# Spacing the first recurrence unit of an encoder kernel, and fixing the place of four scalings in ScalarE's order

## The chip, the cores and the metric

The kernel runs on one core of a Trainium2 chip. The metric is device time in microseconds (us) from the start to the end of one execution. Before the change three runs took 2597.24, 2600.26 and 2603.55 us; the median, 2600.26 us, is the time before.

The engines are named as in the profile: PE is TensorE (matmuls), PEld its weight loads, DVE is VectorE, ACT is ScalarE, POOL is GpSimd, and SP issues the DMAs. Each engine works through its own queue of instructions in order, and waits on semaphores for what other engines produce.

## The reference

One layer of an encoder: 2048 tokens of width 1024, all in float32. What is computed, cut to its core:

```python
h = layernorm(x) * (1 + scale) + shift            # scale, shift, gate from silu(c) @ ada_w + ada_b
proj = h @ w_in                                   # 1024 x 9216
q_h, i_h, zf_fw, zf_bw, g_h, q_n, k_n, v_n, g_n = split(proj)
y_hg = hgrn2(q_h, i_h, zf_fw, zf_bw, g_h)         # gated linear recurrence in both directions, 8 heads of 128
y_na = neighbourhood_attention(q_n, k_n, v_n) * silu(g_n)   # 16 heads of 64
x = layernorm(alpha * x + gate * (concat(y_hg, y_na) @ w_out)) * ln_g + ln_b
```

In the recurrence a state S follows S_t = diag(f_t) S_(t-1) + k_t v_t^T with k = 1 - f, and the output is o_t = S_t^T q_t, once forward and once backward over the tokens.

## The kernel before

**Dense products.** Every product with `w_in` is made of three matmuls in a reduced 32-bit format (line 278): the high part of the weights with the high and the low part of the activations, and the low part of the weights with the high part. One dense *step* is the three matmuls of one 128-row slice of the contraction for one output block of 128 columns by 512 tokens (`proj_mm`); eight steps fill a block. The block then leaves PSUM by a copy or an exponential on ACT (lines 379, 384, 389, 782, 299 and so on), from a pool `pj` of two buffers, so that a block two further on cannot start before that copy. Weights come by DMA into `wr`, ACT rounds them to the high part `wh` (line 268 or 833), DVE subtracts to get the low part `wl` (line 269 or 834). There are four buffers of each.

**Phases that matter here.** After the start, the first half of the tokens (groups 0 and 1 of 512) goes through neighbourhood attention for eight head pairs (`first_half`). Within it, the tokens of the second half (groups g = 0 and 1 of `rows`, `stats`, `scale`, `piece`) are loaded, normalised, transposed and stored for later. This work is laid out by hand in 32 slots, four to a head pair: for g = 0 the loads are in slot 11, the statistics in 12, the two scalings (a = 0 and a = 1, the left and right 512 columns) in 13 and 14, and the eight pieces, which transpose (line 232) and split, from slot 14 on, pieces 0 to 3 using a = 0 and pieces 4 to 7 using a = 1. For g = 1 the statistics and the first scaling are in slot 23, the second scaling and the first piece in 24. One scaling is four instructions: rows 0 and 1 on ACT (line 225), rows 2 and 3 on DVE (line 227).

Then comes the recurrence: 16 units (two token halves by eight heads u), each of two groups g of 512 tokens. While a unit's recurrence is worked, the dense products of the next unit are woven into it.

**What sets the order.** PE's order is the order in which the program is written. `weave` takes a generator of the recurrence (`hgrn`) and one of dense steps; at every `yield w` of the first it issues dense steps until their share of the total has reached the share of the weights so far (a unit has 54 in weights and 80 steps). So the numbers in the `yield` lines 583 to 619 say how many dense steps PE does between two parts of the recurrence. In group 0 of the first unit these are 8, 7, 5, 4, 9 and 8 steps for the weights 5, 5, 3, 3, 6 and 5.

In the two phases above the orders of ACT, DVE and SP are not written out. A planner makes them when the program is built, with costs of its own for every instruction: of what is ready it takes the instruction with the smallest priority number, which is its place in the program, less `PRI` = 1500 inside `tc.high_priority(offset=PRI)`. A change in PE's order therefore makes the plan anew from that point on. `pinned(ins)` adds one rule: `ins` is put behind the instruction that was written last before it on its own engine. In `first_half` the weight roundings of line 833 and the attention's score reductions of line 1065 are so pinned.

**A group of the recurrence, in order.** `turned(vts)` transposes the values; `rates` (ACT and DVE) makes log rates and their running sums for both directions; `ends` makes the factors `de`; `turned(de)` transposes on PE (line 474) and ACT copies the result to `ke` (line 476); `updates(ke, v)` (line 482) makes the state updates, forward then backward; `diagonal_factors` makes `kx` and `qx` (lines 506 to 512), and `diagonal` (line 521) 64 small matmuls with them; `level_factors` and `level` (line 549) do the same for the blocks further from the diagonal; `masked` copies the level's result to `pm` on ACT (line 555), copies the diagonal's result through masks into `pd` on DVE (line 559), and adds the two on DVE (line 562); `outputs` (lines 573 and 575) multiplies with the values and the states.

Of the kernel before, what the change touches and what calls it, by code (L numbers as in the profile page):

```python
# [13 lines left out]
AF = mybir.ActivationFunctionType  # L14
# [16 lines left out]
PRI = 1500  # L31
# [7 lines left out]
def body(ctx: ExitStack, tc: tile.TileContext, t):  # L39
    nc = tc.nc  # L40
    dve, act, pool, pe = nc.vector, nc.scalar, nc.gpsimd, nc.tensor
    dma = nc.sync.dma_start
    x, out = t["x"], t["out"]
# [44 lines left out]
    def nm(s):  # L88
        cnt[0] += 1
        return f"{s}_{cnt[0]}"  # L90

    def tl(tag, dt=F32, shape=None):
        if tag in cur["smap"]:
            tag = cur["smap"][tag]
            return sh.tile([P, 512], dt, tag=tag, name=nm(tag), bufs=SH[tag])
        return cur["pool"].tile([P, 512] if shape is None else shape, dt, tag=tag, name=nm(tag), bufs=cur["bufs"].get(tag, 1))

    def short(dt=F32):
        return tl("s", dt)

    def ps(tag="mx"):
        if tag == "pj":
            return pp.tile([P, 512], F32, tag=tag, name=nm("pj"))
        tag = cur["map"].get(tag, tag)
        return cur["psum"].tile([P, 512], F32, tag=tag, name=nm("ps"), bufs=cur["ps"][tag])
# [109 lines left out]
    def x_stats(xs, pin=lambda x: x):  # L215
        mv = x_mv()
        for i in range(4):
            x_stat(mv, xs, i, pin)
        return x_rates(mv)

    def x_scale(xs, how, a, on_act=2, rows=range(4)):
        mv, r, b = how
        for i in rows:
            if i < on_act:
                act.activation(xs[i][a], xs[i][a], AF.Identity, scale=r[:, i:i + 1], bias=b[:, i:i + 1])
            else:
                dve.tensor_scalar(xs[i][a], xs[i][a], mv[:, i, 0:1], r[:, i:i + 1], op0=ALU.subtract, op1=ALU.mult)

# [135 lines left out]
    def v4(tl, b):  # L364
        return tl.rearrange("p (n c) -> p n c", c=b)
# [57 lines left out]
    def hgrn(u, half, st, tail):  # L423
# [8 lines left out]
        def rates(d, g):  # L432
            col = d * 8 + u
            e = zs[d, g]
            dve.tensor_scalar_min(e, e, ECAP)
            L = tl("g")
            act.activation(L, e, AF.Ln, bias=1.0)
            c = tl("c")
            act.activation(c, e, AF.Ln, scale=lbt[:, col:col + 1], bias=1.0)
            r = tl("g")  # L440
            act.activation(r, L, AF.Exp, scale=-1.0, bias=l1m[:, col:col + 1])
            dve.tensor_tensor(e, e, r, op=ALU.mult)
            for b in range(4):
                lo, hi = b * P, (b + 1) * P
                if d == 0:
                    sl = slice(lo, hi)
                else:
                    sl = slice(hi - 1, lo - 1 if lo else None, -1)
                dve.tensor_tensor_scan(c[:, sl], c[:, sl], L[:, sl], 0.0, op0=ALU.add, op1=ALU.subtract)
            return c, e  # L450
# [20 lines left out]
        def turned(src, tag):  # L471
            pk = ps("tr")
            for b in range(4):
                pe.transpose(pk[:, b * P:(b + 1) * P], src[:, b * P:(b + 1) * P], ident)  # L474
            ke = tl(tag)
            act.activation(ke, pk, AF.Copy)
            return ke

        def updates(ke, v):
            pu = ps("pu")  # L480
            for b in range(4):
                pe.matmul(pu[:, b * P:(b + 1) * P], ke[:, b * P:(b + 1) * P], v[:, b * P:(b + 1) * P], start=True, stop=True)  # L482
            return pu
# [65 lines left out]
                    pe.matmul(pa[s0:s0 + 64, b * P + t0:b * P + t0 + 64], xk[:, b * P + s0:b * P + s0 + 64],  # L549
                              xq[:, b * P + t0:b * P + t0 + 64], start=True, stop=True, skip_group_check=True, tile_position=(0, s0))  # L550

        def masked(pa, pb):

            pm = tl("pm")
            act.activation(pm, pa, AF.Copy)
            pd = pdb[pd_i[0] % 2]
            pd_i[0] += 1
            for m, (o, src) in enumerate(((0, v4(pb[:, 0:256], 64)[:, :, 0:32]), (0, v4(pb[:, 256:384], 32)), (P, v4(pb[:, 0:256], 64)[:, :, 32:64]))):
                dve.copy_predicated(v4(pd[:, o:o + P], 32), msk["mskd"][:, m:m + 1, :].to_broadcast([P, 4, 32]).bitcast(U32), src)
            for j in range(4):  # L560
                sl = slice(j * 32, (j + 1) * 32)
                dve.tensor_tensor(v4(pm, P)[sl, :, sl], v4(pd[sl, 0:P], 32), v4(pd[sl, P:2 * P], 32), op=ALU.add)
            return pm
# [12 lines left out]
            os_[g] = po  # L576

        for g in range(2):
            v = turned(vts[g], "v")
            next(tail, None)  # L580
            cs, ks = {}, {}
            cs[0], ks[0] = rates(0, g)
            yield 5
            next(tail, None)
            cs[1], ks[1] = rates(1, g)
            de0 = ends(0, g, cs[0], ks[0])
            yield 5
            next(tail, None)
            ke0 = turned(de0, "ke")
            de1 = ends(1, g, cs[1], ks[1])  # L590
            kx, qx = diagonal_factors(g, cs, ks)
            yield 3
            next(tail, None)
            pu = updates(ke0, v)
            if u + half + g == 0:
                held = tl("t")
                with tc.high_priority(offset=PRI):
                    act.activation(held, pu, AF.Copy)
                pu = held
            forward_states(g, pu)  # L600
            ke1 = turned(de1, "ke")
            yield 3
            next(tail, None)
            pu = updates(ke1, v)
            if g == 0:
                ub = tl("ub")
                act.activation(ub, pu, AF.Copy)
                ubs[g] = ub
            else:
                ubs[g] = pu  # L610
            pb = diagonal(kx, qx)
            lf = [(w, *level_factors(w, g, cs, ks)) for w in (32, 64)]
            yield 6
            next(tail, None)
            pa = ps("pa")
            for w, xk, xq in lf:
                level(w, pa, xk, xq)
            pm = masked(pa, pb)
            yield 5
            outputs(g, v, pm)  # L620
        for _ in tail:
            pass
# [732 lines left out]
    def first_half(raws, feed, first):  # L1355

        st = Prep(0, 0, raws)
        for n, g in (("k", 0), ("k", 1), ("q", 0), ("g", 0), ("q", 1), ("g", 1)):
            st.piece(n, g)
        for j in (0, 1):  # L1360
            st.table("top", j)
        for c in range(3):
            st.v(c)
        pipe, xs = [], {}

        def rows(g):
            xs[g] = x_load(2 + g)

        how = {}

        def stats(g):
            how[g] = x_stats(xs[g], pinned)

        def scale(g, a):
            x_scale(xs[g], how[g], a)

        def piece(g, k):
            a, b = short(F32R), short(F32R)
            h_piece(xs[g], k, a, b)
            dma(hs[k][:, 0, g * GRP:(g + 1) * GRP], a.bitcast(F32))  # L1380
            dma(hs[k][:, 1, g * GRP:(g + 1) * GRP], b.bitcast(F32))

        slots = {i: [] for i in range(32)}
        slots[0].append((bias_pair, 1))
        for m in range(8):
            slots[2 + m].append((gate_load, m))
            slots[4 + m].append((gate_sum, m))
        slots[5].append((lower_bounds,))
        for g, i in ((0, 11), (1, 22)):
            slots[i].append((rows, g))  # L1390
            slots[i + 1].append((stats, g))
            slots[i + 2 - g].append((scale, g, 0))
            slots[i + 3 - g].append((scale, g, 1))
            for k in range(KT):
                slots[i + 3 - g + k].append((piece, g, k))
        for u in range(2, 8):
            slots[4 * u - 6].append((bias_pair, u))
        for w in range(8):
            extra = {i: slots[4 * w + i] for i in range(4)}
            if w < 7:  # L1400
                nxt = Prep(w + 1, 0, {n: [None, None] for n, _ in NCOL})
                if w == 0:
                    nxt.raws["k"][0] = first
                dense, total, steps = first_stream(nxt, feed), NLEN + (0 if w % 2 == 0 else VLEN) - (0 if w else KT * KUS), 8
            else:
                nxt, dense, total, steps = None, hgrn_dense(0, 0, feed=feed), HTOT, 10
            r = weave(natten_woven(st, nxt, pipe, extra, w == 7), dense, total, steps, ahead=0 if w else AHEAD * KUS)[1]
            st = nxt
        return r
# [42 lines left out]
    with psum_phase("n0", NPS), tc.manual_schedule(engines={mybir.EngineType.PE}):  # L1452
        with phase("st", SB_, SMS), tc.manual_schedule(engines={getattr(mybir.EngineType, e) for e in ("PE", "SP", "Activation", "DVE")}):
            raws, feed, first = startup()
# [10 lines left out]
    with psum_phase("h", *HPS), phase("h", HB, SMH), tc.manual_schedule(engines={mybir.EngineType.PE}):  # L1465
        hgrn_init()
        tail = iter(())
        for i in range(16):
            half, u = divmod(i, 8)
# [136 lines left out]
    with psum_phase("n1", NPS), phase("n1", NB1, SM1), tc.manual_schedule(engines={mybir.EngineType.PE}):  # L1606
# [32 lines left out]
        m, r, c, pts = pipe.pop(0)  # L1639
        m.sums(r, c, pts)  # L1640
        turn(pipe, 1)
        m, r, c, pts = pipe.pop(0)
# [73 lines left out]
```

## Time and profile before

| what | value |
|---|---|
| median of three runs | 2600.26 us (2597.24 to 2603.55) |
| the profiled execution's own time | 2598.38 us |
| its span in the profile | 2596.6 us |
| PE busy | 2556.2 us, 98% |
| DVE busy | 1752.8 us, 68% |
| ACT busy | 1439.6 us, 55% |
| POOL busy | 108.2 us, 4% |
| DMA | 304.79 MB, mean 117 GB/s |
| granted TensorE clock, mean | 0.997 |

The profiled execution took 1.78 us more than its span, and is 1.88 us under the median of the runs. A group's row in the profile reads: line, engine, operation, output <- inputs, shape, count, busy time and mean duration. A row of the timeline reads: start in us from the span's start, duration (of several merged instructions from the first's start to the last's end), engine, line, operation, count, and in brackets how long the engine was idle before it and what released it. A row of the waits reads: who waited for whom, us in total, times, longest. A row of the windows gives the stretch, its length, busy time and count of the engine, the granted PE clock as a share of full speed, and the DMA's share and rate.

### The profile page before, as it was taken

The page shows a single profiled execution, that of the slowest core. Times are in us where ns is not written, and L with a number is a line of the kernel's source. Part 1 is how long each engine was busy: PE and PEld are TensorE (multiplying, and loading weights), DVE is VectorE, ACT ScalarE, POOL GpSimd, SP SyncE. Part 2 cuts the span into 40 slices and gives each one's busy share as a digit, 9 for nine tenths or more (in the row PEclk, how much of TensorE's full clock was granted, in tenths as well). Part 3 has the DMA queues.
Part 4 walks back from the last instruction along what each step waited for, and adds up shares of the span by engine and source line. Part 5 has one row for each costly group of instructions (what it writes and reads, how often), then busy time and mean ns, then how long its engine had stood idle before and what let it go on. Part 6 is the DMA issues. An engine that isn't in the chain of part 4 may idle for free.

```text
span 2596.6 us, 46030 instructions
## 1 busy us (share of the span) xinstructions
PE 2556.2 (98%) x17196; PEld 2151.6 (83%) x17196; DVE 1752.8 (68%) x4394; ACT 1439.6 (55%) x2869; POOL 108.2 (4%) x143
## 2 busy tenths in 40 slices
PE   8999999999999999999999999999999999999998
PEld 6888788878888888888888888898888887788887
DVE  7445545377777778877888787555777778548443
ACT  5533445376666666666766666455777777531110
POOL 0000000000000000000000000000000000032221
PEclk9999999999999999999999999999999999999999
DMA  7566454212122126222222222345455556444331
GB/s 293 142 208 154 140 171 145 91 50 70 66 74 74 66 83 230 83 74 86 77 66 70 82 86 83 120 128 156 125 138 142 145 140 170 133 155 129 96 96 57
DMA packets 230527, 304.79 MB, mean 117 GB/s; under 512 B 29351, under 2 KB 118055, under 8 KB 229159
## 3 DMA queue, kind: packets, MB, share of 16 engines
q1 hardware_dynamic: 230303, 301.85, 38.2%
q8 instruction: 135, 2.21, 0.4%
q14 instruction: 89, 0.73, 0.1%
HBM read 222.37 MB, written 71.18 MB: 113 GB/s over the span
## 4 chain that ended last, share of the span: by engine, by line
PE 92%; DVE 3%; DMA 3%; ACT 1%; issue 0%; SPq 0%; DVEq 0%; ACTq 0%
PE pj L278 51%; PE pj L291 6%; PE ps L1541 4%; PE ps L1543 4%; PE ps L1542 4%; PE ps L1120 3%; PE ps L1098 3%; PE ps L482 2%; PE ps L474 2%; PE ps L1049 1%; PE ps L549 1%; PE ps L573 1%; PE ps L1056 1%; PE ps L521 1%; PE ps L575 1%; PE ps L653 1%
## 5 line engine op out<-in xcount | busy, mean ns | idle before, releaser
L278 PE MATMUL pj<-h,wh 128*128 128x512 f32 x3984 | 1265.4, 399 | 3.6 <-ACT wh L833 1.9
L278 PEld LDWEIGHTS pj<-h,wh 128*128 128x128 f32 x3984 | 722.0, 188 | 152.4 <-issue 10.5
L278 PE MATMUL pj<-h,wl 128*128 128x512 f32 x1992 | 780.6, 392 | 0.0
L278 PEld LDWEIGHTS pj<-h,wl 128*128 128x128 f32 x1992 | 373.9, 188 | 82.9 <-DVE wl L834 0.4
L1070 ACT ACTIVATE pbuf<-pbuf,mx 128x480 f32<-128x480 f32 (+5 forms) x256 | 152.5, 597 | 108.1 <-DVE mx L1065 107.3
L291 PE MATMUL pj<-wh,h 128*128 128x256 f32 x1024 | 196.7, 287 | 2.3 <-ACT vt L299 2.1
L1065 DVE CUSTOM_DVE_ANT_1 pbuf<-ps,bias 128x480 f32<-128x480 f32 (+5 forms) x256 | 129.0, 540 | 96.0 <-PE ps L1056 40.8
L291 PEld LDWEIGHTS pj<-wh,h 128*128 128x128 f32 x1024 | 164.2, 192 | 6.1 <-ACT vt L299 3.4
L269 DVE TENSOR_TENSOR wl<-wr,wh 128x512 fp32r<-128x512 f32 x192 | 131.1, 684 | 46.0 <-ACT wh L268 43.7
L268 ACT ACTIVATE wh<-wr 128x512 fp32r<-128x512 f32 x192 | 120.2, 626 | 72.2 <-PE pj L278 65.9
L291 PE MATMUL pj<-wl,h 128*128 128x256 f32 x512 | 145.3, 284 | 0.0
L1104 ACT ACTIVATE pt<-ps 120x384 f32<-120x384 f32 (+3 forms) x128 | 65.2, 510 | 118.9 <-PE ps L1098 118.6
L1102 DVE COPY pt<-ps 120x384 f32<-120x384 f32 (+3 forms) x128 | 74.9, 585 | 62.7 <-PE ps L1098 61.4
L1098 PE MATMUL ps<-ident,pbuf 128*128 128x128 f32 (+2 forms) x832 | 112.9, 273 | 3.9 <-DVE pbuf L1075 3.0
L1098 PEld LDWEIGHTS ps<-ident,pbuf 128*128 128x128 f32 (+2 forms) x832 | 96.6, 136 | 21.8 <-issue 2.3
L468 DVE TENSOR_TENSOR de<-e,de 128x512 f32<-128x512 f32 x64 | 44.2, 690 | 92.2 <-ACT de L467 92.2
L1517 ACT ACTIVATE yh<-yr 128x512 fp32r<-128x512 f32 x52 | 32.7, 628 | 130.7 <-PE ps L1542 113.6
L1075 DVE TENSOR_SCALAR pbuf<-pbuf,mx 128x480 f32<-128x480 f32 (+5 forms) x256 | 100.9, 412 | 3.8
L1590 DVE TENSOR_TENSOR vt<-ps,gt 128x512 f32<-128x512 f32 x24 | 16.5, 692 | 128.2 <-PE ps L1543 128.2
L782 ACT ACTIVATE e<-pj 128x512 f32<-128x512 f32 x97 | 57.8, 596 | 80.0 <-PE pj L278 73.6
L291 PEld LDWEIGHTS pj<-wl,h 128*128 128x128 f32 x512 | 98.6, 193 | 1.0
L834 DVE TENSOR_TENSOR wl<-wr,wh 128x512 fp32r<-128x512 f32 x68 | 46.7, 690 | 69.2 <-ACT wh L833 68.7
(289 smaller groups left out, 4764.3 us busy)
## 6 DMA issues: line engine op xcount, KB each, us to landing
wr<-in_w_in SPq DMA_DIRECT2D x276, 256.0 KB
yr<-yq SPq DMA_DIRECT2D x64, 256.0 KB
bias<-tint SPq DMA_DIRECT2D x24, 480.0 KB
x<-in_x SPq DMA_DIRECT2D x32, 256.0 KB
ada<-in_ada_m SPq DMA_DIRECT2D x8, 1024.0 KB
wr<-in_w_v SPq DMA_DIRECT2D x32, 256.0 KB
nv<-vt SPq DMA_DIRECT2D x32, 256.0 KB
hs<-s SPq DMA_DIRECT2D x32, 256.0 KB
```

The lines of the kernel that those rows point to most:

```text
L268: act.activation(hi, raw, AF.Copy)
L269: dve.tensor_tensor(lo, raw, hi, op=ALU.subtract)
L278: pe.matmul(pz, a, b, start=(k == 0 and n == 0), stop=(k == KT - 1 and n == 2))
L291: pe.matmul(pzs[tp][:, i * 256:(i + 1) * 256], a, b, start=(k == 0 and n == 0 and i == 0), stop=(k == KT - 1 and n == 2), skip_group_check ...
L1065: return dve.tensor_tensor_reduce(s[:, 0:nk].rearrange("p (r c) -> p r c", c=kw), sc[:, 0:nk].rearrange("p (r c) -> p r c", c=kw), bt[:, 0 ...
L1070: act.activation(s[:, 0:nk], s[:, 0:nk], AF.Exp, scale=-1.0, bias=mx[:, 0:1], accum_out=mx[:, 1:2])
L1075: dve.tensor_scalar(s[:, 0:nk], s[:, 0:nk], mx[:, 2:3], 1.0, op0=ALU.mult, op1=ALU.mult)
L1098: pe.transpose(ptp[0:cw, c * P:(c + 1) * P], s[:, c * cw:(c + 1) * cw], ident)
L1120: pe.matmul(self.po[R][hs_, j * P:(j + 1) * P], v[:, hh * 64:hh * 64 + 64], pts[hh][0:n * KW[j], c * P:(c + 1) * P], start=(c == 0), stop= ...
L1541: pe.matmul(pz, yh[:, kk], wh, start=first, stop=False)
L1542: pe.matmul(pz, yh[:, kk], wl, start=False, stop=False)
L1543: pe.matmul(pz, yl[:, kk], wh, start=False, stop=last)
```

## The change

Two things are changed, and no arithmetic.

1. In group 0 of the first unit (`first`: u + half + g == 0) the weights of the last four `yield` lines go from 3, 3, 6, 5 to 3.5, 6.5, 3, 4. Their sum is the same. Worked out as `weave` does it, the dense steps of that group go from 8, 7, 5, 4, 9, 8 to 8, 7, 6, 9, 5, 6: one more before the forward update, five more before the backward update, four fewer before the level, two fewer before the outputs. In the same group the eight instructions of `masked` get `PRI` priority. In all other groups the offset is 0.
2. In `first_half` the ACT instructions of the scalings (line 225) are pinned, eight in all, and the second scaling (a = 1) of each group moves two slots later: from slot 14 to 16 for g = 0, from 24 to 26 for g = 1. The DVE instructions of the scalings (line 227) move with their slot and are not pinned.

```diff
-    def x_scale(xs, how, a, on_act=2, rows=range(4)):
+    def x_scale(xs, how, a, on_act=2, rows=range(4), pin=lambda x: x):
         mv, r, b = how
         for i in rows:
             if i < on_act:
-                act.activation(xs[i][a], xs[i][a], AF.Identity, scale=r[:, i:i + 1], bias=b[:, i:i + 1])
+                pin(act.activation(xs[i][a], xs[i][a], AF.Identity, scale=r[:, i:i + 1], bias=b[:, i:i + 1]))
...
-        def masked(pa, pb):
+        def masked(pa, pb, first):
 
             pm = tl("pm")
+            with tc.high_priority(offset=PRI if first else 0):
+                return masked_parts(pm, pa, pb)
+
+        def masked_parts(pm, pa, pb):
+
             act.activation(pm, pa, AF.Copy)
...
         for g in range(2):
+            first = u + half + g == 0
...
             kx, qx = diagonal_factors(g, cs, ks)
-            yield 3
+            yield 3.5 if first else 3
             next(tail, None)
             pu = updates(ke0, v)
-            if u + half + g == 0:
+            if first:
                 held = tl("t")
...
             ke1 = turned(de1, "ke")
-            yield 3
+            yield 6.5 if first else 3
             next(tail, None)
             pu = updates(ke1, v)
...
             lf = [(w, *level_factors(w, g, cs, ks)) for w in (32, 64)]
-            yield 6
+            yield 3 if first else 6
...
-            pm = masked(pa, pb)
-            yield 5
+            pm = masked(pa, pb, first)
+            yield 4 if first else 5
             outputs(g, v, pm)
...
         def scale(g, a):
-            x_scale(xs[g], how[g], a)
+            x_scale(xs[g], how[g], a, pin=pinned)
...
             slots[i + 2 - g].append((scale, g, 0))
-            slots[i + 3 - g].append((scale, g, 1))
+            slots[i + 5 - g].append((scale, g, 1))
```

## The prediction

> **What bounds the kernel now.** I read the page first, then PE's waits over the whole span, then the windows around the two places the change touches, and last the timelines there.
>
> ```profile
> span 2596.6 us, 46030 instructions
> PE 2556.2 (98%) x17196; PEld 2151.6 (83%) x17196; DVE 1752.8 (68%) x4394; ACT 1439.6 (55%) x2869; POOL 108.2 (4%) x143
> PE 92%; DVE 3%; DMA 3%; ACT 1%; issue 0%; SPq 0%; DVEq 0%; ACTq 0%
> ```
>
> PE is busy for 98% of the span and makes 92% of the chain that ended last. The change adds and removes no work of PE. So it can only win or lose time in which PE stands still, or in which it runs at a lower clock. The list of PE's waits says where it stands:
>
> ```profile
> PE ps L232 <- ACT x L225: 5.9, 4, 4.5
> PE ps L482 <- ACT ke L476: 3.0, 2, 2.2
> PE pj L278 <- ACT wh L833: 1.9, 1, 1.9
> PE ps L521 <- DVE kx L512: 1.5, 1, 1.5
> ```
>
> The first row names the scaling line that is pinned now, but most of it is the kernel's start, where the scalings have another caller and stay as they are. The second and fourth rows have three waits between them, in 16 units of two groups. The windows show that all three lie in the first unit, and that the clock falls there too (columns: stretch, length, PE busy, granted clock, DMA):
>
> ```profile
> 520.00:545.00 25.00, 23.77 (x121) 1.00 0.20 65
> 545.00:555.00 10.00, 6.35 (x86) 0.83 0.09 28
> 585.00:650.00 65.00, 65.00 (x504) 1.00 0.21 70
> ```
>
> From 585 us on PE is busy without a gap at full clock, so the rest of the recurrence has nothing to win. Here is PE in the first unit, some rows of its timeline:
>
> ```profile
> 539.70 0.39 PE L278 MATMUL pj<-h,wl 128*128 128x512 f32 x1
> 540.90 1.16 PE L482 MATMUL ps<-v,ke 128*128 128x128 f32 x8 [0.81 <-ACT ke L476]
> 542.50 0.70 PE L278 MATMUL pj<-h,wh 128*128 128x512 f32 x2
> 545.12 0.39 PE L278 MATMUL pj<-h,wl 128*128 128x512 f32 x1
> 547.68 1.16 PE L482 MATMUL ps<-v,ke 128*128 128x128 f32 x8 [2.18 <-ACT ke L476]
> 550.31 1.51 PE L521 MATMUL ps<-qx,kx 128*32 128x64 f32 x64 [1.47 <-DVE kx L512]
> 551.75 1.22 PE L278 MATMUL pj<-h,wh 128*128 128x512 f32 x2
> 553.20 0.62 PE L278 MATMUL pj<-h,wh 128*128 128x512 f32 x2
> 557.96 0.61 PE L278 MATMUL pj<-h,wh 128*128 128x512 f32 x2
> 558.73 1.15 PE L549 MATMUL ps<-x,x 128*64 128x64 f32 x32
> 565.39 0.61 PE L573 MATMUL ps<-pm,v 128*128 128x128 f32 x4
> 585.90 0.91 PE L521 MATMUL ps<-qx,kx 128*32 128x64 f32 x64
> ```
>
> Three waits, 0.81 + 2.18 + 1.47 = 4.46 us. Then the same 64 diagonal matmuls take 1.51 us against 0.91 us in the next group: 0.60 us lost to the clock. The next dense step takes 553.20 - 551.75 = 1.45 us. A step at full clock costs (557.96 - 553.20) / 7 = 0.68 us, so 0.77 us more are lost. The first unit thus loses 4.46 + 1.37 = 5.8 us.
>
> **The change part by part: the steps.** One step more stands ahead of the forward update. PE came to it at 539.70 + 0.39 = 540.09 and started at 540.90, when `ke` was there. The step's 0.68 us fits into that wait and leaves 0.13, and the update starts when it did. Five steps more stand ahead of the backward update. PE would come to it at 545.12 + 0.39 + 5 x 0.68 = 548.91. What it waits for next:
>
> ```profile
> 547.04 0.59 ACT L476 ACTIVATE ke<-ps 128x512 f32<-128x512 f32 x1
> 548.98 1.27 DVE L512 TENSOR_TENSOR kx<-kx,e 128x512 f32<-128x512 f32 x2
> 542.31 0.59 ACT L379 ACTIVATE e<-pj 128x512 f32<-128x512 f32 x1
> 548.65 0.60 ACT L379 ACTIVATE e<-pj 128x512 f32<-128x512 f32 x1
> 545.58 0.67 DVE L269 TENSOR_TENSOR wl<-wr,wh 128x512 fp32r<-128x512 f32 x1
> ```
>
> `ke` is ready at 547.63, so the wait of 2.18 us is gone. The update runs to 548.91 + 1.16 = 550.07, and `kx` is ready at 550.25, so the diagonal starts at 550.31 as before, after 0.24 us in place of 1.47: `kx` is what is late next. With 0.13 and 0.24 us of idleness left I expect no fall of the clock. PE then stands at the same moment with six steps more done: 6 x 0.68 = 4.1 us, and with the clock's 1.37 us the gain is 5.4 us. Upwards it ends at 5.8, when `kx` and `ke` come a little sooner. Downwards, ACT and DVE are both full at this time, and one evacuation of 0.60 us placed ahead of the chain to `ke` or `kx` takes 0.6 away: 4.8. I take 5.4, the rows as they are.
>
> The clock's 1.37 us rest on the row of 545 to 555 us, where 0.83 follows on waits of 2.18 and 1.47 us. [...] The trace has only this one fall in the unit, right behind the gaps, so I keep 7.3.
>
> What the extra steps need: the fourth of the nine, at about 544.6, opens the buffer of PSUM that the evacuation at 542.31 clears at 542.90, 1.7 us ahead. The next block, the third step after the diagonal, starts at about 552.6 and needs the evacuation at 548.65, done at 549.25, and the weight part that DVE finishes at 546.25. The weight DMAs are issued with priority and their buffers are filled that far ahead, so SP's queue adds nothing.
>
> **Fewer steps behind.** Four fewer before the level and two fewer before the outputs take away cover. The diagonal ends at 551.2, five steps bring the level to 554.6, and six steps after its 1.15 us bring the outputs to 559.9. They need `pm`. Three rows, of ACT, DVE and ACT:
>
> ```profile
> 559.93 0.60 ACT L555 ACTIVATE pm<-ps 128x512 f32<-128x512 f32 x1
> 563.82 1.17 DVE L562 TENSOR_TENSOR pm<-pdb 32x128 f32<-32x128 f32 x4
> 556.15 1.06 ACT L508 ACTIVATE qx<-kx 128x1024 f32<-128x1024 f32 x1 [0.83 <-DVE kx L506]
> ```
>
> Before, DVE's additions came 3.3 us after ACT's copy, behind other work, and were done at 564.99, just ahead of the outputs at 565.39. At that distance (level 558.73, `pm` 564.99: 6.3 us) the outputs would now wait 554.6 + 6.3 - 559.9 = 1.0 us. The priority is there to close it: the copy of 0.60 and the additions of 1.17 us, and at worst 1.06 us of ACT and the 1.27 us of `kx` on DVE running ahead of them, make 4.1 us after the level's end, and six steps are 4.1 us. So I cost this at nothing; without the priority it costs 1.0 us. The priority of 0 in the other 31 groups takes nothing away from a number, and I cost it at nothing.
>
> **The scalings.** The other wait, of 1.9 us, in the rows of PE and ACT:
>
> ```profile
> 262.54 0.82 PE L1098 MATMUL ps<-ident,pbuf 128*96 128x128 f32 x6
> 268.00 0.74 PE L278 MATMUL pj<-h,wh 128*128 128x512 f32 x2 [1.90 <-ACT wh L833]
> 262.51 2.92 ACT L225 ACTIVATE x<-x,xb,xr 128x512 f32<-128x512 f32 x4
> 265.34 0.58 ACT L299 ACTIVATE vt<-pj 128x512 f32<-128x512 f32 x1
> 265.81 0.58 ACT L1070 ACTIVATE pbuf<-pbuf,mx 128x352 f32<-128x352 f32 x1
> 266.96 0.47 ACT L1104 ACTIVATE pt<-ps 96x384 f32<-96x384 f32 x1
> 267.33 1.67 ACT L833 ACTIVATE wh<-wr 128x512 fp32r<-128x512 f32 x3
> 286.35 0.60 PE L232 MATMUL ps<-ident,x 128*128 128x128 f32 x4
> 423.42 0.86 PE L232 MATMUL ps<-ident,x 128*128 128x128 f32 x4
> ```
>
> All four scalings of g = 0 sit in one block of 2.92 us ahead of an evacuation, a pair of powers, a copy and the weights for which PE waits at 268.00. Their first reader is at 286.35, 18 us later. In the program the last ACT instruction written before the first scaling is the copy of the transposes (line 1104), and the weight roundings stand before that. So the pinned pair cannot be issued ahead of the copy, and the second pair is two slots away. Without the block the weights come up to 2.92 us sooner, more than the 1.90 that is waited: gain 1.9. If the planner puts the pinned pair straight behind the copy and still ahead of the weights, half of the block stays and 2.92 / 2 = 1.46 is won. I take 1.9, because the roundings have the better place in the program. The pair costs the same ACT time later, where ACT waits for scores; who is queued behind it there has its inputs no sooner. For g = 1 the first pair is pinned behind the rates it needs anyway, and the piece at 423.42 (0.86 against 0.60 us) keeps its 0.26. The second pair leaves ACT free for 1.46 us there, with nothing on PE waiting for it: nothing. The DVE halves move without a reader near, and no DMA is moved.
>
> **The sum.** 5.4 + 1.9 = 7.3 us. The profiled execution's 2598.38 becomes 2591.1; it lies 1.9 under the median of the runs, and from the median, 2600.26, I forecast 2593.0 us. What a measurement of this kernel can tell from no change is about 0.2%, 5.2 us, so the gain is 2.1 us over that line.
>
> **The rivals.**
>
> *The wait moves to `pm` or to PSUM inside the first unit.* The planner's order is made with its own costs, and in this stretch ACT and DVE have no idle time. If the masked additions stay behind other DVE work, or the evacuation that ran at 542.31 slips by more than 1.7 us, PE waits again, and with a second low clock the 5.4 us are used up. For it speaks that this evacuation already came 5 us after its block; against it, that both have priority. Time: 2600.26 - 1.9 = 2598.4.
>
> *The pin does not help.* The pinned pair still delays the weights, or another copy does, and only the first unit gains: 2600.26 - 5.4 = 2594.9. Against it speaks the order in the program.
>
> *The clock is not won back.* The low clock has another cause than the waits and stays, and 1.4 us with it: 2600.26 - 5.9 = 2594.4. The rows speak against it: the fall comes right behind 3.65 us of waiting within 4.8, and there is none in the stretch from 585 us, where there are no gaps. [...]
>
> *Slower: the new plan brings waits into the groups that had none.* From 262 us on ACT and DVE are planned anew, and after the first unit PE runs 5.4 us closer behind them. One wait of the smallest size seen, 0.81 us, in each of the other 31 groups costs 25.1 us: 2600.26 - 7.3 + 25.1 = 2618.1. From 7.3 / 31 = 0.24 us a group it eats the gain, from 12.5 / 31 = 0.40 the kernel is slower by over 0.2%. Against it: the window from 585 us shows PE full while DVE and ACT are at 68% and 55% of the span.
>
> **How the numbers follow.** My forecast 0.56, with a range of its own of 2590 to 2595.5; clock 0.05; pin 0.07; first unit 0.18; slower 0.14. Forecast, clock and pin give a gain over 5.2 us with 0.54, 0.04 and 0.04: faster 0.62. The rest of these (0.06) and nearly all of the first unit's rival (0.17) are within 0.2%: 0.23. Slower is the last rival and the tail of the first: 0.15. The low end is the upper gain, 7.7 us, and the runs' own scatter of 3 us below the median: 2589.5. The high end takes in the first unit's rival and 2 us of scatter: 2600.5. Outside lie the slower case and small tails.
>
> **What would show it.** Right: in PE's waits, line 482 on `ke` falls from 3.0 to under 0.3, line 521 on `kx` to under 0.5, the row `wh` of line 833 is gone; the window with the first unit's diagonal has clock 1.00, and its 64 matmuls take about 0.9 us; ACT shows two scalings of 1.46 us behind line 1104 in place of four. Wrong: a wait of line 573 on `pm`, a wait of line 278 on `e` of line 379, or waits of PE in the recurrence after the first unit.

## The result, and the profile after

The changed kernel takes 2598.12 us (median of 14 runs, 2594.98 to 2600.51) against 2601.30 us (14 runs, 2595.73 to 2604.96). The ratio is 0.9984, with a 95% interval of 0.9977 to 0.9991: a gain of 4.2 us, between 2.3 and 6.0; the medians themselves differ by 3.2 us. I had forecast 7.3 us and 2593.0 us. The time lies in the range, the direction is right, and the gain is a little over half of what was forecast, so it falls within 0.2%. The median is nearer to the 2598.4 us of the first rival than to the forecast.

The page's first lines, and the rows of PE's waits that belong to the change:

```profile
span 2594.5 us, 46029 instructions
PE 2557.3 (99%) x17196; PEld 2154.2 (83%) x17196; DVE 1752.1 (68%) x4394; ACT 1438.9 (55%) x2869; POOL 108.5 (4%) x143
```

```profile
PE ps L232 <- ACT x L225: 7.1, 4, 5.6
PE ps L578 <- ACT x L539: 2.8, 1, 2.8
PE ps L521 <- DVE kx L512: 0.5, 1, 0.5
```

The rows for `ke` (3.0 us before) and for `wh` (1.9 us before) are gone, and the one for `kx` fell from 1.5 to 0.5. But there is a new row of 2.8 us: line 578, which was 573, the outputs. Here is PE in the first unit, to be laid beside the rows of before:

```profile
540.13 1.16 PE L482 MATMUL ps<-v,ke 128*128 128x128 f32 x8
547.99 1.06 PE L482 MATMUL ps<-v,ke 128*128 128x128 f32 x8
549.55 0.91 PE L521 MATMUL ps<-qx,kx 128*32 128x64 f32 x64 [0.50 <-DVE kx L512]
554.02 1.15 PE L549 MATMUL ps<-x,x 128*64 128x64 f32 x32
558.63 0.62 PE L278 MATMUL pj<-h,wh 128*128 128x512 f32 x2
562.28 1.19 PE L578 MATMUL ps<-pm,v 128*128 128x128 f32 x4 [2.80 <-ACT x L539]
565.39 0.76 PE L474 MATMUL ps<-ident,vt 128*128 128x128 f32 x4
```

Up to the level everything came as forecast: both updates start at once, and the diagonal takes 0.91 us in place of 1.51. Then the last dense step ends at 559.5 and the outputs start at 562.28. They also run slowly, 3.11 us up to the next transposes against 1.57 before (565.39 to 566.96). Of the two blocks, the first is the row of before at which that stretch ends. The second is from windows of half a microsecond of the changed kernel, and the number behind the bracket is the granted clock:

```profile
566.96 0.60 PE L474 MATMUL ps<-ident,vt 128*128 128x128 f32 x4
```

```profile
562.00:562.50 0.50, 0.22 (x1) 0.79 0.00 0
562.50:563.00 0.50, 0.50 (x3) 0.50 0.00 0
565.50:566.00 0.50, 0.50 (x6) 0.80 0.00 0
```

The low clock that was to go is there again, behind the new wait. What were the outputs waiting for? These are ACT and DVE of the changed kernel:

```profile
556.47 0.58 ACT L560 ACTIVATE pm<-ps 128x512 f32<-128x512 f32 x1
557.14 0.42 DVE L534 TENSOR_TENSOR x<-c 128x256 f32<-128x256 f32 x1
558.82 1.23 DVE L510 TENSOR_TENSOR qx<-qx,q 128x1024 f32<-128x1024 f32 x1
560.96 1.17 DVE L567 TENSOR_TENSOR pm<-pdb 32x128 f32<-32x128 f32 x4
```

ACT's copy to `pm` is done at 557.05. DVE's four additions start 3.9 us later, behind the eight subtractions of the next group's level factors (the row at 557.14 is the first) and the product for `qx`. They end at 562.13. The waits' row names ACT's line 539, which ended at about the same time (562.17); the additions are what the outputs read, and two experiments below move them.

The scalings went as forecast. In the changed kernel ACT and PE do this near 266 us, and the last row is of PE before:

```profile
266.45 1.66 ACT L839 ACTIVATE wh<-wr 128x512 fp32r<-128x512 f32 x3
268.02 1.51 ACT L225 ACTIVATE x<-x,xb,xr 128x512 f32<-128x512 f32 x2
264.25 0.82 PE L1104 MATMUL ps<-ident,pbuf 128*96 128x128 f32 x6
269.69 0.32 PE L1055 MATMUL ps<-KA,q 128*128 128x352 f32 x1
```

```profile
270.46 0.32 PE L1049 MATMUL ps<-KA,q 128*128 128x352 f32 x1
```

The weights now come ahead of the scalings, and only two scalings stand in the block. From the transposes of line 1104 (1098 before) to the next scores PE needs 5.44 us, where before it needed 270.46 - 262.54 = 7.92. That is 2.5 us, not 1.9.

The two built programs differ little in their order: a few dozen instructions on ACT, DVE and SP stand elsewhere, none on POOL. So the fear that everything behind would be planned anew had no ground here.

### The profile page after: what moved, and what is told of

The parts are those of the page before. It is cut to its first block, busy times and chain, and to the rows that moved or that the text cites. A ratio compares the mean times of both kernels' runs of the same rounds, so it can differ in the third digit from the quotient of the medians.

```text
span 2594.5 us, 46029 instructions
## 1 busy us (share of the span) xinstructions
PE 2557.3 (99%) x17196; PEld 2154.2 (83%) x17196; DVE 1752.1 (68%) x4394; ACT 1438.9 (55%) x2869; POOL 108.5 (4%) x143
## 4 chain that ended last, share of the span: by engine, by line
PE 94%; DVE 3%; ACT 1%; DMA 1%; issue 0%; SPq 0%; DVEq 0%; ACTq 0%
PE pj L278 51%; PE pj L291 7%; PE ps L1549 4%; PE ps L1547 4%; PE ps L1548 4%; PE ps L1126 3%; PE ps L1104 3%; PE ps L482 2%; PE ps L474 2%; PE ps L1055 2%; PE ps L549 1%; PE ps L278 1%; PE ps L578 1%; PE ps L1062 1%; PE ps L580 1%; PE ps L521 1%
```

## The experiments

Ratios are to the kernel before, on the same chip. Diffs are to the changed kernel, except where they say otherwise. "Undone" means the lines of before.

### Each part alone

`pins_only`: yields and priority undone. `steps_only`: pins and slots undone.

```diff
 pins_only
-            yield 3.5 if first else 3
+            yield 3
-            yield 6.5 if first else 3
+            yield 3
-            yield 3 if first else 6
+            yield 6
-            yield 4 if first else 5
+            yield 5
-            with tc.high_priority(offset=PRI if first else 0):
+            with tc.high_priority(offset=0):
 steps_only
-            x_scale(xs[g], how[g], a, pin=pinned)
+            x_scale(xs[g], how[g], a)
-            slots[i + 5 - g].append((scale, g, 1))
+            slots[i + 3 - g].append((scale, g, 1))
```

> The second part of the change alone: scalings pinned and their second halves two slots later; the yields of the first unit and the masked additions as before the change. In the changed kernel's trace the stretch from the transposes of line 1104 (1098 before) to the next scores took 5.44 us against 7.92, so this part is worth 2.5 us wherever it runs: time 2.5 us under the kernel before, ratio 0.9990, with no wait of PE for the weights of line 839 and the first unit's three waits (0.8, 2.2, 1.5 us) as before. Rival: the part only pays together with the other, or moves its wait elsewhere: ratio 1.000.

> The first part alone: the new yields and the priority in the first unit; scalings as before the change. Theory (the queue): the three waits at ke and kx go, but the outputs wait 2.8 us for the masked additions, which stand in DVE's order behind eight subtractions and a product of the next group, and the clock halves behind that wait; from the transposes of the values to the first dense step behind the outputs 41.9 us against 42.5, a gain of 0.6 us, ratio 0.9998. Rival (the forecast's term holds and was lost elsewhere, by the pins): a gain of 5.4 us, ratio 0.9979.

Measured: `pins_only` 0.9980 (0.9971 to 0.9989), `steps_only` 0.9997 (0.9988 to 1.0006). By these times the gain is the pins', 5.2 us (2.9 to 7.5), more than the 2.5 us that I expected of them. The steps bring 0.8 us (between -1.6 and 3.1), nothing that can be told from zero. The traces, PE in `steps_only`, then in `pins_only`:

```profile
269.58 0.73 PE L278 MATMUL pj<-h,wh 128*128 128x512 f32 x2 [1.90 <-ACT wh L839]
270.64 0.97 PE L278 MATMUL pj<-h,wh 128*128 128x512 f32 x2
566.10 0.68 PE L578 MATMUL ps<-pm,v 128*128 128x128 f32 x4 [2.82 <-ACT x L539]
```

```profile
545.33 2.06 PE L482 MATMUL ps<-v,ke 128*128 128x128 f32 x8 [2.18 <-ACT ke L476]
```

In `steps_only` the wait of 2.82 us at the outputs is there without any low clock (0.68 for the first four matmuls, against 1.19 in the changed kernel). But the old wait of 1.90 us for the weights, with no low clock behind it before, is followed by one here: a pair of dense matmuls takes 0.97 us in place of 0.62. In `pins_only` the low clock already holds in the update (2.06 against 1.16 us). Whether a wait comes with the low clock differs from one profile to the next: 1.90 us at the weights had none before and have it here, 2.80 us at the outputs have it in the changed kernel and 2.82 us here have none.

### Is it DVE's order? Additions put ahead, and more cover

`adds_first` orders the next group's eight subtractions behind the additions of the first group, on the same engine; it adds no wait. The rule names the last of the four additions, not the first. `more_cover` leaves the order and moves four dense steps from group 1 to the place ahead of the outputs.

```diff
 adds_first
+        adds = []
+        def behind_adds(ins):
+            if u + half == 0 and adds:
+                tc.add_manual_dep(ins.ins, adds[0].ins.name, ...)   # NoSync: order only
+            return ins
...
-            dve.tensor_tensor(xkv[:, :, 0, :], rf, cv[0][:, :, 0, :], op=ALU.subtract)
+            behind_adds(dve.tensor_tensor(xkv[:, :, 0, :], rf, cv[0][:, :, 0, :], op=ALU.subtract))
...
-                dve.tensor_tensor(v4(pm, P)[sl, :, sl], ...)
+                last_add = dve.tensor_tensor(v4(pm, P)[sl, :, sl], ...)
+            adds.append(last_add)
...
 more_cover
-            yield 4 if first else 5
+            yield 7 if first else 4 if u + half == 0 else 5
-            yield 3 if first else 6
+            yield 3 if first else 5 if u + half == 0 else 6
             cs[0], ks[0] = rates(0, g)
-            yield 5
+            yield 4 if u + half == 0 and g else 5
```

> The changed kernel with one more rule for the planner: in the first unit the subtractions of the level factors of the next group are issued behind the first masked addition (order alone, no wait is added or taken, the same work on the same engines). Theory (DVE's order makes the outputs late): copy done at about 557.1, the additions behind the one product that is left ahead of them, done at about 559.5; the outputs wait under 0.3 us instead of 2.8, the clock stays at 1.00, and the time is 4.3 us under the changed kernel: ratio to the kernel before 0.9970 to 0.9975. Rival (the additions are late because the level and its copy are late, cover being too small in itself): wait stays at 2 us or more, ratio as the changed kernel's, 0.9984.

> The changed kernel with ten dense steps in place of six between level and outputs of group 0 of the first unit, and four fewer in group 1 of that unit (weights 4, 5, 3, 3, 5, 4 there). The additions end when they did; PE comes to the outputs 4 x 0.68 = 2.7 us later with that much more done. Theory (a wait of 2.8 us and then the low clock is all that was lost): wait under 0.3 us, clock 1.00, time 2.7 + 1.6 = 4.3 us under the changed kernel, ratio 0.9970 to 0.9975. Rival (ACT and DVE are behind by a fixed amount, and the wait only moves into group 1, which now has four steps fewer): a wait of 1 us or more in group 1, ratio 0.9980 to 0.9985.

Measured: `adds_first` 0.9967 (0.9955 to 0.9980), 2593.54 us; `more_cover` 0.9968 (0.9956 to 0.9980), 2594.58 us. Both as the queue theory had it. DVE and PE in `adds_first`, with the window behind:

```profile
556.68 1.21 DVE L510 TENSOR_TENSOR qx<-qx,q 128x1024 f32<-128x1024 f32 x1
557.82 1.16 DVE L574 TENSOR_TENSOR pm<-pdb 32x128 f32<-32x128 f32 x4
559.01 0.42 DVE L534 TENSOR_TENSOR x<-c 128x256 f32<-128x256 f32 x1
559.13 0.68 PE L586 MATMUL ps<-pm,v 128*128 128x128 f32 x4
```

```profile
555.00:565.00 10.00, 9.86 (x53) 8.21 (x52) 9.93 (x25) 6.63 (x13) 0.00 (x0) 1.00 0.16 55
```

Only the `qx` product is still ahead of the additions. They end at 558.98 and the outputs follow without a wait, at full clock. DVE's busy time in the window is 9.93 of 10 us (the third of the busy times in the row), the same as in the changed kernel: nothing became faster, the order changed. In `more_cover` the outputs also start without a wait, and of the feared wait in group 1 there is 0.56 us:

```profile
592.14 0.46 PE L578 MATMUL ps<-pm,v 128*128 128x128 f32 x2 [0.56 <-DVE pm L567]
```

`adds_first` is 8.6 us faster than the kernel before by its ratio, and 4.4 us faster than the changed kernel (0.9984, 0.9977 to 0.9991), though these two intervals still touch.

### Another engine for the additions

```diff
-                dve.tensor_tensor(v4(pm, P)[sl, :, sl], ...)
+                (pool if pd_i[0] == 1 else dve).tensor_tensor(v4(pm, P)[sl, :, sl], ...)
```

> The changed kernel with the four masked additions of the first group on POOL, which is idle then, in place of DVE. Theory (DVE's order makes the outputs late): the additions start when the copy is done, at about 557.1, take about 1.5 us on POOL, and the outputs at 559.3 wait under 0.3 us; ratio to the kernel before 0.9967 to 0.9972, as with the additions put ahead on DVE. Rival (the copy or the masked copies are late themselves): wait of 1 us or more, ratio 0.998.

Measured: 0.9998 (0.9989 to 1.0007). POOL, and PE's wait:

```profile
556.70 9.11 POOL L567 TENSOR_TENSOR pm<-pdb 32x128 f32<-32x128 f32 x4 [37.84 <-ACT pm L560]
```

```profile
PE ps L578 <- POOL pm L567: 6.9, 1, 6.9
```

The expected time failed: I had put four additions on POOL at 1.5 us, an estimate for which I had no row, and they took 9.1. The profile's times on POOL are rough, but PE's wait ends with them (565.86 against 556.70 + 9.11 = 565.81). And the row answers what was asked. POOL starts at 556.70, released by ACT's copy, so all inputs of the additions were there at that moment, at which DVE went on with the eight subtractions.

### Does the priority do anything?

```diff
-            with tc.high_priority(offset=PRI if first else 0):
+            with tc.high_priority(offset=0):
```

> The changed kernel without the priority of the masked part in the first group. Theory (what is late for the planner is not made earlier by priority): the same wait of 2.8 us at the outputs and the same order on DVE, ratio as the changed kernel's, 0.9984; whether the clock falls behind the wait may differ from one execution to the next. Rival (the priority brings the additions forward, and without it they come later still): a wait of 3.5 us or more.

Measured: 0.9985 (0.9975 to 0.9994), the changed kernel's value, and the same wait; the clock falls here 0.8 us behind the row's start:

```profile
560.08 0.68 PE L578 MATMUL ps<-pm,v 128*128 128x128 f32 x4 [2.79 <-ACT x L539]
```

The built program has the same order as the changed kernel's on every engine. The priority chooses among instructions that are ready in the planner's own reckoning. Why the additions come so late in that reckoning stays open.

### The pin or the move

`pin_no_move`: as `pins_only`, with the second scaling back in its old slot (`i + 3 - g`).

> The pins of the scalings alone, all four scalings of a group staying in the slots of before. Theory (the pin is what frees the weights): no wait of PE for the weights of line 839 at 266 to 268 us, ratio as with both, 0.9980. Rival (the move of the second half is what counts): the wait of 1.9 us or most of it is still there, ratio 0.9995 to 1.000.

Measured: 0.9989 (0.9979 to 0.9998). The interval holds both 0.9980 and 0.9995, so the times don't decide; the trace does:

```profile
263.97 0.82 PE L1104 MATMUL ps<-ident,pbuf 128*96 128x128 f32 x6
269.41 0.32 PE L1055 MATMUL ps<-KA,q 128*128 128x352 f32 x1
```

Again 5.44 us, and no wait for the weights. The move without the pin was not run; the program built from it has the order of before on every engine, row for row. So the pin is what counts.

### The clock, by itself

`keep_warm` puts 40 matmuls of the identity with itself ahead of the outputs, `keep_warm11` puts 11 there. If the low clock comes of PE standing still, the outputs behind them run at full clock.

```diff
             po = ps("po")
+            if u + half + g == 0:
+                for _ in range(11):
+                    pe.matmul(po[:, 0:P], ident, ident, start=True, stop=True, skip_group_check=True)
```

> The changed kernel with 40 matmuls of the identity with itself in PE's order straight ahead of the outputs of the first group, into the buffer that the outputs then overwrite; they need nothing that is late, so PE works through part of the 2.8 us in which it waited. [...] Rival (the fall of the clock has another cause than the gap): the clock is still 0.5 for 3.4 us behind it, ratio 0.9984 or above.

> As the run with 40 identity matmuls, with 11: those 40 took 9.1 us (80 passes of 0.11 us), so 11 take 2.5 us and fit into the wait of 2.8 us. Theory (the clock falls because PE stands still): the outputs start when they did, the wait left is about 0.3 us, and no half clock follows: 0 to 1.5 us under the changed kernel, as that one does or does not fall to half clock in an execution; ratio 0.9978 to 0.9985. Rival (the fall has another cause than the gap): 3.4 us at half clock behind the wait.

Measured: `keep_warm` 0.9991 (0.9982 to 1.0000), `keep_warm11` 0.9967 (0.9955 to 0.9979). PE's rows, first of the run with 40, then of that with 11:

```profile
557.99 9.10 PE L575 MATMUL ps<-ident 128*128 128x128 f32 x80
```

```profile
559.56 2.62 PE L575 MATMUL ps<-ident 128*128 128x128 f32 x22
562.51 0.68 PE L581 MATMUL ps<-pm,v 128*128 128x128 f32 x4 [0.33 <-ACT x L539]
```

Forty were far too many: each shows as two records of 0.11 us, 9.1 us in all, so that run paid more than the wait. With eleven the additions still end late, PE is busy meanwhile, and the outputs run at full clock (0.68 against 1.19 us). In its profile the stretch between the transposes of values of groups 0 and 1 is 39.91 us against 41.39, 1.5 us less. The measured ratio shows more than that; the interval, 6 runs wide, reaches from 5.5 to 11.7 us under the kernel before, and the trace does not explain what lies beyond the 1.5 us.

### The first term alone

`steps_adds_first`: `adds_first` with pins and slots undone.

> The first part of the change alone, with the masked additions put ahead of the next group's subtractions in DVE's order; scalings as before the change. It measures the forecast's first term by itself. Theory (the steps are worth what the waits and the low clock cost, once the additions are in time): from the transposes of the values to those of the next group 37.2 us against 42.2, 5.0 us, ratio 0.9975 to 0.9985, and the wait for the weights at 268 us as before. Rival (the gain of the additions put ahead belongs to the pins or to chance): ratio 0.9997 as with the steps alone.

Measured: 0.9975 (0.9965 to 0.9984), a gain of 6.5 us (4.2 to 9.1), as the theory had it: with the additions in time the steps are worth what I had forecast for them, 5.4. The additions put ahead without the steps were not run; before, the outputs had no wait that this could have removed.

### All profiles by stretches

A is the start of the transposes near 263 us (line 1098 of the kernel before, whose number shifts with the edits), B the transposes of the values of group 0 of the first unit, C those of group 1 (line 474). "Half clock" is the time at half clock from A to 10 us behind C, summed over windows of half a microsecond. Times in us.

| kernel | start to A | A to B | B to C | half clock |
|---|---|---|---|---|
| before | 262.54 | 262.23 | 42.19 | 3.41 |
| `pins_only` | 262.68 | 259.74 | 42.84 | 6.82 |
| `pin_no_move` | 263.97 | 259.77 | 43.64 | 6.83 |
| after | 264.25 | 259.75 | 41.39 | 3.41 |
| `no_priority` | 262.08 | 259.74 | 40.63 | 3.41 |
| `steps_only` | 264.12 | 263.70 | 39.92 | 3.41, all near 272 us |
| `steps_adds_first` | 263.16 | 263.73 | 37.24 | 3.41, all near 271 us |
| `adds_first` | 263.77 | 259.76 | 37.23 | 0 |
| `more_cover` | 262.37 | 259.76 | 39.92, four more steps in it | 0 |
| `keep_warm` | 262.92 | 259.76 | 45.81, 9.1 us of identity in it | 0 |
| `keep_warm11` | 264.49 | 259.75 | 39.91 | 0 |
| `adds_pool` | 263.76 | 259.75 | 45.50 | 10.24 |

With the pins, A to B is 259.74 to 259.77 in all nine profiles. Without them it is 262.23 or, where the low clock follows the wait for the weights, 263.7: mean 263.2, so the pins are worth 3.5 us. B to C has a mean of 42.9 with the old steps (42.19, 42.84, 43.64), and 37.2 with the additions put ahead. With the new steps it is 41.39, 40.63 and 39.92, but in the first two 0.3 and 1.9 us of the half clock lie behind C. If half of that is lost, an estimate, they become 41.5 and 41.6, and the mean is 41.0. That makes 3.5 + 1.9 = 5.4 us for the changed kernel, within its 2.3 to 6.0, and 3.5 + 5.7 = 9.2 us for `adds_first`, ratio 0.9965 against 0.9967 measured. The start, which no edit touches, varies by 2.4 us from one profile to the next, so single profiles' spans are no measure of 4 us.

## Why the prediction was right or wrong

**The number: in part luck.** The 2598.12 us lie outside the 2590 to 2595.5 that I gave the forecast itself, and inside the whole range because it took in the first rival. And two errors partly offset each other: the steps brought 0.8 us by the times and 1.9 by the stretches in place of 5.4, the scalings 5.2 and 3.5 in place of 1.9.

**The steps ahead: right.** Both updates lost their waits. `kx` was late next, as forecast, with 0.50 us in place of 0.24: the update ran 1.06 us and not 1.16. With the additions put ahead as well, `steps_adds_first` puts the term at 6.5 us with an interval that holds the forecast 5.4.

**"Fewer steps behind ... I cost this at nothing": this step failed.** It rested on the priority to bring the additions close behind the copy, and the priority changes nothing in the order. The other price I named, 1.0 us without priority, was too low as well. I had carried over the 6.3 us from the level to the finished `pm` as if the level set the additions' time. It doesn't: DVE is full there (busy 9.93 us of the 10 from 555 us on), and the additions come when DVE has worked off what stands ahead of them. I had allowed 1.27 us of DVE's work ahead of them; behind the copy it did 3.8 us of other work first (557.14 to 560.96). These are the values' transposes, before and after:

```profile
524.77 0.66 PE L474 MATMUL ps<-ident,vt 128*128 128x128 f32 x4
524.00 0.66 PE L474 MATMUL ps<-ident,vt 128*128 128x128 f32 x4
```

Counted from them, the additions ended 564.99 - 524.77 = 40.2 us later before and 562.13 - 524.00 = 38.1 after, 2.1 us sooner, while PE came to the outputs over 5 us sooner. The wait was 2.8 us, with the low clock behind it (3.11 - 1.57 = 1.5 us) 4.3 us in the profiled execution: that is most of what the term of 5.4 us lacks.

**The clock: the cause right, the sum wrong.** The low clock did come with the waits: of seven profiles with a wait of PE of 2 us or more in the first unit six have it there, of the five without such a wait (such as `adds_first` and `keep_warm11`) none. But the changed kernel has a wait of its own and with it the low clock again, in two of three profiles of this wait. It came with 2.80 us of waiting in the changed kernel and behind 1.90 us in `steps_only`; the 1.90 us of before and the 2.82 us of `steps_only` had none. Where it came it lasted 3.41, 6.82 or 6.83, and 10.24 us (the table). What decides whether a wait has it, no run shows.

**The scalings: right in mechanism, too small in size.** The scalings are issued behind the copy of line 1104 (1110 now) and behind the weights, as the program's order said. The term was 1.9 us; the profile gives 2.5 and the mean over profiles 3.5 (`pins_only` by its times 5.2, 2.9 to 7.5), because the wait of 1.9 us is in two of the three profiles that have it followed by a low clock (`steps_only` and `steps_adds_first`, 3.41 us each). I had looked for the low clock only in the first unit.

**The rivals.** The wait that moves to `pm` is what happened, for most of the first unit's gain; I gave it 0.18. Its price of all 5.4 us was a little high, by the stretches (5.4 - 1.9 = 3.5). That the pin doesn't help fell with `pins_only`. The slower case, waits in the other 31 groups, fell with the profile after, where PE has no wait in the recurrence behind the first unit that was not there before, and with the orders, which changed in few rows.

## What to carry to other kernels

When the busiest engine is spread out so that one wait goes, look at the order of the engine that makes the next input, not at its distance. Here DVE was busy 9.93 of 10 us, its additions came 3.9 us behind the copy because of what stood ahead of them in its order, and the six steps of cover taken from there came back as a wait of 2.80 us. The priority changed nothing in the built order here; compare the order with and without it before counting on it. Order alone, eight small instructions put behind four, took the ratio from 0.9984 to 0.9967 here, about as much as the whole change.

## What the runs showed of the hardware that I had not expected

From 250 to 600 us, PE's clock fell to 0.50 in or just behind waits of 1.47 to 2.80 us (6.91 us in `adds_pool`), for 3.41, 6.82, 6.83 or 10.24 us, and not in every profile of the same wait: 3 profiles with the wait of 2.8 us had 3.41, 3.41 and 0 us of it with that wait. The wait of 1.90 us for the weights cost 1.5 us more where the low clock followed it (A to B 263.70 us in `steps_only` against 262.23 before). And four additions of 32x128 elements took 9.11 us on POOL (`adds_pool`) against 1.17 on DVE (the changed kernel).
